# Values' product of two attentions: the two heads of a pair alternate block by block

## The chip, the cores and the metric

One core of a Trainium2 chip runs the kernel. The metric is the device time of one execution in microseconds (us); lower is better. Before the change the median of three runs is 2707.13 us (2704.09 to 2709.62).

## The reference

Two layers on a sequence of 1024 tokens of width 1024, in float32. Each has two token mixers; the change touches one of either layer. In the first layer it is the stick-breaking attention, eight heads of width 64, query blocks of 128:

```
z = jnp.einsum('bhqd,bhkd->bhqk', q[:, :, q0:end], k[:, :, :end]) * scale
mask = kj < qi
log_keep = jnp.where(mask, jax.nn.log_sigmoid(-z), 0.0)
rest = lax.cumsum(log_keep, axis=3, reverse=True) - log_keep
a = jnp.where(mask, jnp.exp(jax.nn.log_sigmoid(z) + rest), 0.0)
outs.append(jnp.einsum('bhqk,bhkd->bhqd', a, v[:, :, :end]))
```

In the second layer it is a softmax attention with low-rank queries and keys, again eight heads with values of width 64:

```
logits = jnp.einsum('bhqd,bhkd->bhqk', qb, k_t).astype(jnp.float32) * scale
logits = jnp.where(allowed[None, None], logits, NEG_INF)
probs = jax.nn.softmax(logits, axis=-1).astype(v_t.dtype)
return jnp.einsum('bhqk,bhkd->bhqd', probs, v_t)
```

Both end in a product of weights and values: the change rewrites how that product is ordered. The rest (a gated delta rule, a differential attention, a gated feed-forward part, projections and norms) stays as it is.

## The kernel before, in words

The program is one list of instructions per engine. A scheduler orders each list when the kernel is built, from the order of the code, the dependencies and its own costs; on the chip every engine works through its list in order. TensorE's order therefore has projections, scores, transposes and values' products mixed.

The stick-breaking attention is `sb` (line 822 on), the softmax attention of the second layer `mla` (line 1159 on). Both call `attend` (line 790), which walks over a list of items from `pairs` (line 885): for each of four pairs of heads `p` and eight query blocks `i`, one item with both heads where `i < 4`, and two items with one head each from `i = 4` on. For item `n`, `attend` first runs `s0` of that item and then `s1` of the item two places earlier. `s0` multiplies queries with keys into a PSUM tile `z` (two of them, each of two banks) and makes the weights: in `sb` three ScalarE passes, a VectorE pass, a VectorE scan, a VectorE subtraction and an exponential, into `cs`; in `mla` a maximum on VectorE, an exponential on ScalarE and a scaling on GpSimd, into `e`. `s1` calls `attend_pv` (line 889), which multiplies the weights with the values.

`attend_pv` needs the weights with keys on the partitions. It transposes them on TensorE, 128 by 128, up to four blocks into one PSUM bank `pt` (line 903), copies the bank to the SBUF tile `aT` (line 904: VectorE in `sb`; in `mla` ScalarE for an item's first chunk and VectorE for the others), and after all chunks of the item multiplies (line 907): 128 keys by 64 value columns as weights, 128 queries streamed. Head 0 of the pair goes to partitions 0 to 63 of the PSUM tile `po`, head 1 to 64 to 127. The blocks are in the order of heads first: all key blocks of head 0, then all of head 1. With `i` 0 or 1 both heads fit one chunk; with `i` 2 and 3 each head has a chunk of its own; from `i = 4` on each head is an item of its own. PSUM's eight banks hold two for projections (`pj`), one `pt`, four for `z` and one `po`.

Beside these attentions `mix` runs a second stream of work: next to `sb` the projections of `proj_z` (512-column products into `pj`), next to `mla_proj` and `mla` the query and key projections of the third attention, `diff_proj`. That one uses `qk_stack` (line 717), whose inner `stack` (line 741) transposes a projected tile (line 747), casts it to `qb_st` on ScalarE and subtracts on VectorE (helper `split_evac`, lines 301 and 302), and stores it to `dr_dqk` (line 750). `qk_stack` runs twice: in `proj_b` in the pool `pb`, and in `diff_proj` in the pool `self.fp`.

Of the kernel before, what the change touches and what calls it, by code (L numbers as in the profile page):

```python
# [11 lines left out]
F32 = mybir.dt.float32  # L12
F32R = mybir.dt.float32r
# [10 lines left out]
NT = 8  # L24
# [127 lines left out]
class Kern:  # L152
# [564 lines left out]
    def qk_stack(self, pool, xn, ws, gains, dst):  # L717


        nc = self.nc  # L720

        def proj(gi, half, w):
            raw = pool.tile([128, 4, 256], F32, tag="qb_raw", name="qb_raw", bufs=2)
            rv = raw.rearrange("p t (h f) -> p (t h) f", h=4)
            ss = pool.tile([128, 16], F32, tag="qb_ss", name="qb_ss", bufs=2)
            for j in range(2):
                ps = self.tm(w, xn, 8, 2 * half + j).rearrange("p j (h f) -> p (j h) f", h=4)
                sq = pool.tile([128, 8, 64], F32, tag="qb_sq", name="qb_sq", bufs=1)
                nc.scalar.activation(sq, ps, AF.Square)
                nc.vector.tensor_tensor(rv[:, 8 * j:8 * j + 8, :], ps, gains[gi // 2][:, None, :].to_broadcast([128, 8, 64]), ALU.mult)  # L730
                nc.vector.reduce_sum(ss[:, 8 * j:8 * j + 8], sq, axis=AX.X)
                yield
            if gi < 2:

                r = self.rsqrt(ss, 16, 1.0, 64 * EPS)
            else:
                r = self.rsqrt(ss, 16, 1.0 / 64, EPS)
            nc.gpsimd.tensor_tensor(rv, rv, r[:, :, None].to_broadcast([128, 16, 64]), ALU.mult)
            self.stack_raw = raw

        def stack(gi, half, raw):
            for pr in range(2):
                p = 2 * (gi % 2) + pr
                st = pool.tile([128, 2, 512], F32R, tag="qb_st", name="qb_st", bufs=2)
                pt = self.PT()
                for j in range(4):
                    nc.tensor.transpose(pt[:, j, :], raw[:, j, pr * 128:pr * 128 + 128], self.ident)
                self.split_evac(st[:, 0], st[:, 1], pt.rearrange("p a b -> p (a b)"))
                a = 2 * (gi // 2)
                nc.sync.dma_start(dst[p, :, a:a + 2, half * 512:half * 512 + 512], st.bitcast(F32))  # L750
                yield

        pend = None
        for gi in range(4):
            w = self.W(ws[gi])
            for half in range(2):
                yield from proj(gi, half, w)
                if pend:
                    yield from stack(*pend)
                pend = gi, half, self.stack_raw  # L760
        yield from stack(*pend)

    def load_qk(self, pool, src, half):
# [58 lines left out]
    def sb(self):  # L822
        nc, d, tc = self.nc, self.d, self.tc
        mm = nc.tensor.matmul
        es = ExitStack()
        sp = es.enter_context(self.pool("sbp", 1, "right"))
        pz = es.enter_context(self.pool("sbz", 2, space=PSUM))
        po_ = es.enter_context(self.pool("sbo", 1, space=PSUM))
        st = {}
# [7 lines left out]
        def s0(p, i, hs):  # L837
# [8 lines left out]
            nk = (i + 1) * 128  # L846
# [3 lines left out]
            for a, h in enumerate(hs):  # L850
                for c0 in range(0, nk, 512):
                    n = min(512, nk - c0)
# [6 lines left out]
            new = lambda tag, bufs: sp.tile([128, 1024], F32, tag=tag, name=tag, bufs=bufs)[:, :len(hs) * nk].rearrange("p (a k) -> p a k", a=len(hs))  # L859
            e = new("e", 2)  # L860
# [2 lines left out]
            nc.scalar.activation(e, e, AF.Exp, scale=-1.0)  # L863
            nc.scalar.activation(e, e, AF.Ln, bias=1.0)
            nc.vector.scalar_tensor_tensor(e, zz, 0.0, e, ALU.max, ALU.add)
            cs = new("cs", 4)
            for a in range(len(hs)):
                nc.vector.tensor_tensor_scan(cs[:, a, ::-1], self.ones[:, 0:1].to_broadcast([128, nk]), e[:, a, ::-1], 0.0, ALU.mult, ALU.add)  # L868
            nc.vector.tensor_tensor(cs, zz, cs, ALU.subtract)
# [1 line left out]
            st[p, i, hs] = cs  # L871

        def s1(p, i, hs):
            cs = st.pop((p, i, hs))
            qk, v, ob = st[p]
            po = self.attend_pv(sp, po_, st, cs, v, i, hs, nc.vector.tensor_copy, nc.vector.tensor_copy)
            if hs[-1] == 1:
                nc.vector.tensor_copy(ob[:, i * 128:i * 128 + 128], po)
                if i == NT - 1:
                    nc.sync.dma_start(self.dr_oa[1, :, p, :], ob)  # L880

        yield from self.attend(self.pairs(), s0, s1)
        es.close()

# [1 line left out]

        return [(p, i, hs) for p in range(4) for i in range(NT) for hs in ([(0, 1)] if i < 4 else [(0,), (1,)])]

    def attend_pv(self, sp, po_, st, e, v, i, hs, *copy):

        nc = self.nc
        mm = nc.tensor.matmul
        if hs[0] == 0:
            st["po"] = po_.tile([128, 128], F32, tag="po", name="po")
        po = st["po"]
        blocks = [(a, j) for a in range(len(hs)) for j in range(i + 1)]
        aT = sp.tile([128, 8, 128], F32, tag="aT", name="aT", bufs=2)
        step = 4 if i != 2 else 3
        for b0 in range(0, len(blocks), step):
            pt = self.PT()  # L900
            bs = blocks[b0:b0 + step]
            for b, (a, j) in enumerate(bs):
                nc.tensor.transpose(pt[:, b, :], e[:, a, j * 128:j * 128 + 128], self.ident)  # L903
            copy[b0 > 0](aT[:, b0:b0 + len(bs), :], pt[:, :len(bs), :])  # L904
        for b, (a, j) in enumerate(blocks):
            h = hs[a]
            mm(po[64 * h:64 * h + 64, :], v[:, j, h * 64:h * 64 + 64], aT[:, b, :], start=j == 0, stop=j == i)  # L907
        return po

    def merge_in(self):  # L910
# [248 lines left out]
    def mla(self):  # L1159
        nc, d, tc = self.nc, self.d, self.tc  # L1160
        mm = nc.tensor.matmul
        es = ExitStack()
        sp = es.enter_context(self.pool("mla", 1, "right"))
        pz = es.enter_context(self.pool("mlaz", 2, space=PSUM))
        po_ = es.enter_context(self.pool("mlao", 1, space=PSUM))
        st = {}
# [14 lines left out]
        def s0(p, i, hs):  # L1181
# [7 lines left out]
            nk = (i + 1) * 128  # L1189
            q = slice(i % 4 * 128, i % 4 * 128 + 128)  # L1190
            z = pz.tile([128, len(hs), 1024 // len(hs)], F32, tag="z", name="z")
            for a, h in enumerate(hs):
                qk = st[p][0]
                qt = qk[h, 0, i // 4]
                for c0 in range(0, nk, 512):
                    n = min(512, nk - c0)
# [5 lines left out]
            zz = z[:, :, :nk]  # L1202
            nm, s, r = (self.small.tile([128, 2], F32, tag=f"a_{n}", name=f"a_{n}", bufs=4)[:, :len(hs)] for n in "msr")
            nc.vector.reduce_max(nm, zz, axis=AX.X, negate=True)
            e = sp.tile([128, 1024], F32, tag="e", name="e", bufs=3)[:, :len(hs) * nk].rearrange("p (a k) -> p a k", a=len(hs))
            for a in range(len(hs)):
                nc.scalar.activation(e[:, a], zz[:, a], AF.Exp, bias=nm[:, a:a + 1], accum_out=s[:, a:a + 1])
            nc.vector.reciprocal(r, s)
# [2 lines left out]
            st[p, i, hs] = e  # L1211

        def s1(p, i, hs):
            e = st.pop((p, i, hs))
            qks, v = st[p]
            po = self.attend_pv(sp, po_, st, e, v, i, hs, nc.scalar.copy, nc.vector.tensor_copy)
            if hs[-1] == 1:
                if i % 4 == 0:
                    st["ob"] = sp.tile([128, 512], F32, tag="ob", name="ob", bufs=1)
                nc.vector.tensor_copy(st["ob"][:, i % 4 * 128:i % 4 * 128 + 128], po)  # L1220
                if i % 4 == 3:
                    nc.sync.dma_start(self.dr_mix[:, p, (i - 3) * 128:(i + 1) * 128], st["ob"])

        yield from self.attend(self.pairs(), s0, s1)
        es.close()

# [448 lines left out]
```

## Time and profile before

| | us |
|---|---|
| median of three runs | 2707.13 |
| lowest, highest | 2704.09, 2709.62 |
| the profiled execution | 2711.15 |
| its span | 2709.3 |
| TensorE matmul busy in the span | 2548.5 (94%) |
| VectorE busy | 1461.3 (54%) |
| ScalarE busy | 864.7 (32%) |
| GpSimd busy | 1057.1 (39%) |
| share of the chain that ended last: TensorE | 61% |

Times of single instructions are from the profiled execution, in us from the start of its span unless marked ns. PE is TensorE's matmul, PEld its weight load, DVE VectorE, ACT ScalarE, POOL GpSimd, SP the engine that issues DMAs. A float32 matmul of the program leaves two records in the trace, one after the other, each with a weight load of its own; the records of a transpose are one each. Matmuls are pipelined, so a record lasts longer than the step to the next: what a matmul costs is read from start to start.

### The profile page before, as it was taken

The numbers are of one execution on the slowest core, as the hardware profiler recorded it, in microseconds if no ns is written. First come the engines' busy times: TensorE is split into PE (matmuls) and PEld (weight loads), VectorE is DVE, ScalarE is ACT, GpSimd is POOL, SyncE is SP. The second block draws the span as 40 slices with busy tenths as digits, with TensorE's granted clock in tenths as the row PEclk, the third lists the DMA queues.
The fourth block names the chain that finished last, engine by engine and source line by source line (L and its number), as shares of the span: only waits on it lengthen the run. The fifth ranks groups of instructions, "written<-read, shape, count | busy, mean of one in ns | idle before, by whom it ended". The sixth has DMA issues, their size and how long they took to land.

```text
span 2709.3 us, 38990 instructions
## 1 busy us (share of the span) xinstructions
PE 2548.5 (94%) x15298; PEld 2173.9 (80%) x15298; DVE 1461.3 (54%) x2837; ACT 864.7 (32%) x1575; POOL 1057.1 (39%) x920
## 2 busy tenths in 40 slices
PE   6998999999999989999889998889999999999999
PEld 6888888877777768989777787788777777777789
DVE  6565565275666554457844336666454454534372
ACT  3322222154444342122324335463333333201031
POOL 2533332122122234544533232223677777634322
PEclk9999999999999999999989999999999999999999
DMA  4433223153421355322674337554122222523222
GB/s 155 132 103 107 79 86 101 56 142 97 119 86 63 133 175 190 105 82 82 207 200 128 94 123 171 170 186 156 55 79 70 86 85 64 196 83 109 70 82 90
DMA packets 152335, 311.46 MB, mean 115 GB/s; under 512 B 14132, under 2 KB 57396, under 8 KB 152152
## 3 DMA queue, kind: packets, MB, share of 16 engines
q1 hardware_dynamic: 152152, 308.97, 36.7%
q8 instruction: 121, 1.98, 0.3%
q14 instruction: 62, 0.51, 0.1%
HBM read 211.91 MB, written 99.37 MB: 115 GB/s over the span
## 4 chain that ended last, share of the span: by engine, by line
PE 61%; DVE 10%; DMA 5%; ACT 3%; issue 2%; POOL 1%; SPq 0%; ACTq 0%; DVEq 0%; POOLq 0%
PE pj L1525 15%; PE pj L254 10%; PE pj L253 10%; PE pj L252 10%; PE po L907 5%; PE pt L903 3%; DMA dr_mla<-l_st 1%; PE po L1333 1%; PE z L253 1%; DVE cs L868 1%; PE z L252 1%; DMA m_o<-dr_oa 1%; DVE rs_a L293 1%; PE z L254 1%; DVE rs_a L292 1%
## 5 line engine op out<-in xcount | busy, mean ns | idle before, releaser
L243 POOL TENSOR_SCALAR hl<-raw 128x512 fp32r<-128x512 f32 (+3 forms) x270 | 197.6, 737 | 961.0 <-PE pj L254 949.5
L244 POOL TENSOR_TENSOR hl<-raw,hl 128x512 fp32r<-128x512 f32 (+3 forms) x270 | 368.7, 1371 | 16.0
L252 PE MATMUL pj<-hl,xn_0h 128*128 128x256 f32 (+2 forms) x544 | 160.6, 296 | 2.3 <-DVE qb_st L302 1.1
L253 PE MATMUL pj<-hl,xn_0h 128*128 128x256 f32 (+2 forms) x544 | 160.6, 295 | 1.7 <-POOL hl L244 1.7
L252 PE MATMUL pj<-hl,xn_1h 128*128 128x256 f32 (+2 forms) x544 | 159.2, 293 | 0.0
L254 PE MATMUL pj<-hl,xn_1l 128*128 128x256 f32 (+2 forms) x544 | 158.8, 292 | 0.0
L254 PE MATMUL pj<-hl,xn_0l 128*128 128x256 f32 (+2 forms) x544 | 158.7, 292 | 0.0
L253 PE MATMUL pj<-hl,xn_1h 128*128 128x256 f32 (+2 forms) x544 | 158.3, 291 | 0.0
L1506 POOL TENSOR_TENSOR hl<-w_s,hl 128x512 fp32r<-128x512 f32 x88 | 120.9, 1375 | 84.1 <-ACT hl L1505 84.0
L907 PE MATMUL po<-aT,v 128*64 128x128 f32 x1152 | 150.4, 280 | 2.2 <-DVE aT L904 1.6
L254 PE MATMUL pj<-hl,f_hl 128*128 128x512 f32 x352 | 140.4, 401 | 2.9 <-DVE f_hl L1607 2.9
L252 PE MATMUL pj<-hl,f_hh 128*128 128x512 f32 x352 | 140.0, 398 | 2.9 <-DVE xres L1616 2.4
L907 PEld LDWEIGHTS po<-aT,v 128*64 128x64 f32 x1152 | 116.5, 136 | 30.6 <-issue 19.2
L253 PE MATMUL pj<-hl,f_hh 128*128 128x512 f32 x352 | 138.3, 393 | 0.0
L1616 DVE TENSOR_TENSOR xres<-xres,pj 128x512 f32<-128x512 f32 x96 | 65.1, 685 | 126.2 <-PE pj L254 113.2
L1506 POOL TENSOR_TENSOR hl<-raw,hl 128x512 fp32r<-128x512 f32 x66 | 100.2, 1524 | 70.4 <-ACT hl L1505 69.7
L904 DVE COPY aT<-pt 128x512 f32<-128x512 f32 (+3 forms) x128 | 72.5, 566 | 99.2 <-PE pt L903 99.0
L1561 DVE TENSOR_TENSOR f_u<-pj,w_u 128x512 f32<-128x512 f32 x44 | 30.4, 692 | 169.1 <-ACT w_u L1529 96.3
L252 PE MATMUL pj<-xn_0h,hl 128*128 128x512 f32 x288 | 116.8, 406 | 0.0
L252 PE MATMUL pj<-xn_1h,hl 128*128 128x512 f32 x288 | 115.7, 402 | 0.0
L254 PE MATMUL pj<-xn_1h,hl 128*128 128x512 f32 x288 | 114.9, 399 | 0.0
L253 PE MATMUL pj<-xn_1l,hl 128*128 128x512 f32 x288 | 114.8, 399 | 0.0
(599 smaller groups left out, 7436.8 us busy)
## 6 DMA issues: line engine op xcount, KB each, us to landing
raw<-in_w_o_dram SPq DMA_DIRECT2D x28, 512.0 KB, 4.3
dr_mla<-l_st SPq DMA_DIRECT2D x32, 384.0 KB, 3.7
qk<-dr_mla SPq DMA_DIRECT2D x32, 384.0 KB, 4.8
raw<-in_w_fg_dram SPq DMA_DIRECT2D x22, 512.0 KB, 4.5
raw<-in_w_fu_dram SPq DMA_DIRECT2D x22, 512.0 KB, 3.5
dr_h<-f_y SPq DMA_DIRECT2D x22, 512.0 KB, 5.3
raw<-in_w_fd_dram SPq DMA_DIRECT2D x22, 512.0 KB, 3.8
f_y<-dr_h SPq DMA_DIRECT2D x22, 512.0 KB, 4.2
```

Of the source, the lines that this page charges most:

```text
L243: nc.gpsimd.tensor_scalar(hl[:, 0], raw[:, k:k + c], 1.0, 1.0, ALU.mult, ALU.mult)
L244: nc.gpsimd.tensor_tensor(hl[:, 1], raw[:, k:k + c], hl[:, 0].bitcast(F32), ALU.subtract)
L252: mm(ps, lh[0], rh[0], start=first, stop=False)
L253: mm(ps, lh[0], rh[1], start=False, stop=False)
L254: mm(ps, lh[1], rh[0], start=False, stop=last)
L903: nc.tensor.transpose(pt[:, b, :], e[:, a, j * 128:j * 128 + 128], self.ident)
L904: copy[b0 > 0](aT[:, b0:b0 + len(bs), :], pt[:, :len(bs), :])
L907: mm(po[64 * h:64 * h + 64, :], v[:, j, h * 64:h * 64 + 64], aT[:, b, :], start=j == 0, stop=j == i)
L1506: nc.gpsimd.tensor_tensor(hl[:, 1], v, hl[:, 0].bitcast(F32), ALU.subtract)
L1525: nc.tensor.matmul(ps, w[k][l], b[r][:, k, :], start=first and k + n == 0, stop=k == 3 and n == 2, skip_group_check=not first)
L1561: nc.vector.tensor_tensor(u, ps, v, ALU.add)
L1616: nc.vector.tensor_tensor(xr, xr, ps, ALU.add)
```

## The change

`attend_pv` takes both heads of a pair at once. Where the heads are items of their own, `s1` does nothing for the first and handles both with the second. The loop goes over key blocks two at a time; a chunk holds those two blocks of both heads, head 0 and head 1 in turn, in one PSUM bank. Each chunk has its own small `aT` tile (four blocks; five buffers in `sb`, four in `mla`, where there were two of eight blocks), and its products follow directly in the code, again with heads in turn. Since more weights are held at a time, `cs` goes from four to five buffers and `e` of `mla` from three to four; to make room, `qb_st` has one buffer in the pool `self.fp` and still two in the other. The line numbers move by one or two: 903 becomes 904 and 907 becomes 908.

```diff
         def stack(gi, half, raw):
...
-                st = pool.tile([128, 2, 512], F32R, tag="qb_st", name="qb_st", bufs=2)
+                st = pool.tile([128, 2, 512], F32R, tag="qb_st", name="qb_st", bufs=1 if pool is getattr(self, "fp", None) else 2)
...
-            cs = new("cs", 4)
+            cs = new("cs", 5)
...
         def s1(p, i, hs):
-            cs = st.pop((p, i, hs))
+            if hs == (0,):
+                return
             qk, v, ob = st[p]
-            po = self.attend_pv(sp, po_, st, cs, v, i, hs, nc.vector.tensor_copy, nc.vector.tensor_copy)
-            if hs[-1] == 1:
-                nc.vector.tensor_copy(ob[:, i * 128:i * 128 + 128], po)
+            po = self.attend_pv(sp, po_, st, v, p, i, 5, nc.vector.tensor_copy, nc.vector.tensor_copy)
+            nc.vector.tensor_copy(ob[:, i * 128:i * 128 + 128], po)
...
-    def attend_pv(self, sp, po_, st, e, v, i, hs, *copy):
+    def attend_pv(self, sp, po_, st, v, p, i, bufs, *copy):
         nc = self.nc
-        mm = nc.tensor.matmul
-        if hs[0] == 0:
-            st["po"] = po_.tile([128, 128], F32, tag="po", name="po")
-        po = st["po"]
-        blocks = [(a, j) for a in range(len(hs)) for j in range(i + 1)]
-        aT = sp.tile([128, 8, 128], F32, tag="aT", name="aT", bufs=2)
-        step = 4 if i != 2 else 3
-        for b0 in range(0, len(blocks), step):
+        if i < 4:
+            both = st.pop((p, i, (0, 1)))
+            e = [both[:, a] for a in range(2)]
+        else:
+            e = [st.pop((p, i, (a,)))[:, 0] for a in range(2)]
+        po = po_.tile([128, 128], F32, tag="po", name="po")
+        for j0 in range(0, i + 1, 2):
+            blocks = [(j, a) for j in range(j0, min(j0 + 2, i + 1)) for a in range(2)]
+            n = len(blocks)
             pt = self.PT()
-            bs = blocks[b0:b0 + step]
-            for b, (a, j) in enumerate(bs):
-                nc.tensor.transpose(pt[:, b, :], e[:, a, j * 128:j * 128 + 128], self.ident)
-            copy[b0 > 0](aT[:, b0:b0 + len(bs), :], pt[:, :len(bs), :])
-        for b, (a, j) in enumerate(blocks):
-            h = hs[a]
-            mm(po[64 * h:64 * h + 64, :], v[:, j, h * 64:h * 64 + 64], aT[:, b, :], start=j == 0, stop=j == i)
+            for b, (j, a) in enumerate(blocks):
+                nc.tensor.transpose(pt[:, b, :], e[a][:, j * 128:j * 128 + 128], self.ident)
+            aT = sp.tile([128, 4, 128], F32, tag="aT", name="aT", bufs=bufs)
+            copy[j0 > 0](aT[:, :n], pt[:, :n])
+            for b, (j, a) in enumerate(blocks):
+                nc.tensor.matmul(po[64 * a:64 * a + 64, :], v[:, j, a * 64:a * 64 + 64], aT[:, b, :], start=j == 0, stop=j == i)
         return po
...
-            e = sp.tile([128, 1024], F32, tag="e", name="e", bufs=3)[:, :len(hs) * nk].rearrange("p (a k) -> p a k", a=len(hs))
+            e = sp.tile([128, 1024], F32, tag="e", name="e", bufs=4)[:, :len(hs) * nk].rearrange("p (a k) -> p a k", a=len(hs))
...
         def s1(p, i, hs):
-            e = st.pop((p, i, hs))
+            if hs == (0,):
+                return
             qks, v = st[p]
-            po = self.attend_pv(sp, po_, st, e, v, i, hs, nc.scalar.copy, nc.vector.tensor_copy)
-            if hs[-1] == 1:
...
+            po = self.attend_pv(sp, po_, st, v, p, i, 4, nc.scalar.copy, nc.vector.tensor_copy)
```

The scheduler's order changes with it. TensorE in `sb`, near query block 6 of the first pair, before (`pj` is a projection product, `pt` a chunk of transposes, `po` values' products; x4 counts matmuls of the program):

```order
L252 MATMUL pj<-xn_0h,hl 128x512
L903 MATMUL pt<-cst,cs 128x128 x3
L907 MATMUL po<-aT,v 64x128 x4
L253 MATMUL pj<-xn_0l,hl 128x512
L254 MATMUL pj<-xn_0h,hl 128x512
L252 MATMUL pj<-xn_0h,hl 128x512
L907 MATMUL po<-aT,v 64x128 x3
```

and now:

```order
L904 MATMUL pt<-cst,cs 128x128 x4
L252 MATMUL pj<-xn_1h,hl 128x512
L253 MATMUL pj<-xn_1l,hl 128x512
L254 MATMUL pj<-xn_1h,hl 128x512
L252 MATMUL pj<-xn_1h,hl 128x512
L908 MATMUL po<-aT,v 64x128 x4
L904 MATMUL pt<-cst,cs 128x128 x4
```

Before, the products of one head's chunks stand in runs of up to eight matmuls; now a run is one chunk of four (or two), with four or five projection products between its transposes and its products.

TensorE at the end of `mla` (`z` are the scores, `identb` loads the weights for the mask's product), now:

```order
L904 MATMUL pt<-cst,e 128x128 x4
L252 MATMUL z<-qk 128x512
L253 MATMUL z<-qk 128x512
L254 MATMUL z<-qk 128x512
L1202 LDWEIGHTS identb
L1202 MATMUL z<-negch,identb 128x64
L908 MATMUL po<-aT,v 64x128 x4
L904 MATMUL pt<-cst,e 128x128 x4
L908 MATMUL po<-aT,v 64x128 x4
L904 MATMUL pt<-cst,e 128x128 x4
```

Three score products and a mask stand between transposes and products, and after the last scores nothing does. Before, projection products of the next phase stand in this place.

ScalarE in the first pair of `qb_st` casts beside `mla_proj`, before:

```order
L301 CAST qb_st<-pt 128x512 x2
L304 ACTIVATE qlT0h<-pt,g_ql 128x512 x2
L304 ACTIVATE kvT0h<-pt,g_kvl 128x512
L729 ACTIVATE qb_sq<-pj 128x512
```

and now:

```order
L301 CAST qb_st<-pt 128x512
L304 ACTIVATE qlT0h<-pt,g_ql 128x512 x2
L304 ACTIVATE kvT0h<-pt,g_kvl 128x512
L301 CAST qb_st<-pt 128x512
L729 ACTIVATE qb_sq<-pj 128x512
```

The second cast has moved behind three other evictions, ahead of `qb_sq`.

## Rows read from the trace of the kernel before

**Rows 1.** Busy us of each engine by stretch, with counts; granted clock, DMA share, GB/s.

```profile
554.00:914.00 360.00, 353.58 (x1949) 272.91 (x1948) 240.56 (x293) 162.57 (x203) 77.15 (x72) 1.00 0.32 93
1230.00:1413.00 183.00, 156.04 (x1151) 148.60 (x1150) 130.64 (x344) 56.01 (x117) 79.22 (x64) 0.94 0.57 169
1413.00:1628.00 215.00, 212.22 (x1501) 170.68 (x1501) 85.88 (x178) 83.09 (x190) 63.82 (x82) 0.99 0.39 117
```

**Rows 2.** The chain of waits by line, at 554 to 914, then 1413 to 1628.

```profile
by line: PE po L907 18.2%; PE pj L253 15.2%; PE pj L254 15.0%; PE pj L252 14.6%; PE pt L903 8.8%; DVE cs L868 5.3%; PE z L855 4.1%; PE z L856 4.0%; DVE e L865 2.8%; issue 2.1%; ACT e L862 1.9%; ACT e L864 1.7%; DVE cs L869 1.5%; DVE aT L904
...
by line: PE po L907 32.2%; PE pt L903 17.8%; PE z L253 9.0%; PE z L252 8.3%; PE z L254 7.4%; PE pj L253 5.2%; PE pj L252 4.9%; PE pj L254 4.8%; DMA dr_mix<-ob 2.4%; PE z L1201 1.5%; POOL hl L244 1.2%; POOL hl L243 1.1%; PE pt L747 1.0%; ACT
```

**Rows 3.** Instructions by shape, 554 to 914: records | busy us, mean ns | idle before.

```profile
L907 PE MATMUL po<-aT,v 128*64 128x128 f32 x576 | 75.5, 280 | 1.6 <-DVE aT L904 1.6
```

**Rows 4.** Timeline, one head's run and a copy: start, length, engine, instruction, records.

```profile
572.11 0.60 PE L903 MATMUL pt<-cst,cs 128*128 128x128 f32 x4
572.64 1.09 PE L907 MATMUL po<-aT,v 128*64 128x128 f32 x8
573.66 0.39 PE L856 MATMUL z<-k,q 128*128 128x256 f32 x1
...
572.75 0.69 DVE L904 COPY aT<-pt 128x512 f32<-128x512 f32 x1 [0.65 <-PE pt L903]
```

**Rows 5.** Timeline of TensorE, the runs of query blocks 0 and 1.

```profile
555.91 0.44 PE L907 MATMUL po<-aT,v 128*64 128x128 f32 x4
556.28 0.50 PE L252 MATMUL pj<-xn_1h,hl 128*128 128x512 f32 x1
...
559.35 0.40 PE L252 MATMUL pj<-xn_1h,hl 128*128 128x512 f32 x1
559.58 0.39 PE L253 MATMUL pj<-xn_1l,hl 128*128 128x512 f32 x1
559.90 0.66 PE L907 MATMUL po<-aT,v 128*64 128x128 f32 x8
560.50 0.50 PE L254 MATMUL pj<-xn_1h,hl 128*128 128x512 f32 x1
```

**Rows 6.** Timeline of the weight loads of the two runs of eight.

```profile
559.90 0.42 PEld L907 LDWEIGHTS po<-aT,v 128*64 128x64 f32 x8 [0.36 <-issue]
...
572.64 0.85 PEld L907 LDWEIGHTS po<-aT,v 128*64 128x64 f32 x8 [0.17 <-issue]
```

**Rows 7.** Copies of four blocks, by shape: 554 to 914, then 1413 to 1628.

```profile
L904 DVE COPY aT<-pt 128x512 f32<-128x512 f32 x52 | 35.7, 686 | 32.3 <-PE pt L903 32.2
...
L904 ACT COPY aT<-pt 128x512 f32<-128x512 f32 x40 | 23.4, 586 | 73.5 <-PE pt L903 68.2 <-issue 3.7 <-PE z L1201 1.6
```

**Rows 8.** Waits on the copies, us, times, longest: 554 to 914, then 1413 to 1628.

```profile
PEld pt L903 <- DVE aT L904: 11.9, 28, 1.3
PEld po L907 <- DVE aT L904: 4.3, 8, 1.3
PE pt L903 <- DVE aT L904: 3.6, 6, 0.9
...
PEld pt L903 <- ACT aT L904: 6.5, 25, 0.5
PE pt L903 <- ACT aT L904: 1.1, 3, 0.4
```

**Rows 9.** Casts and stores of `qb_st`, timeline; last the DMA's median us to landing.

```profile
1237.28 1.07 ACT L301 CAST qb_st<-pt 128x512 fp32r<-128x512 f32 x2
...
1241.42 0.94 SPq L750 DMA_DIRECT2D dr_dqk<-qb_st  x2
...
1260.71 0.36 SPq L750 DMA_DIRECT2D dr_dqk<-qb_st  x1
...
1261.24 0.59 ACT L301 CAST qb_st<-pt 128x512 fp32r<-128x512 f32 x1 [2.00 <-PE pt L747]
...
dr_dqk<-qb_st SPq DMA_DIRECT2D x16, 512.0 KB, 4.4
```

More of the change, by code (lines that the diff above doesn't have):

```diff
@@ L873, in s1 @@
         def s1(p, i, hs):
-            cs = st.pop((p, i, hs))
+            if hs == (0,):
+                return
             qk, v, ob = st[p]
-            po = self.attend_pv(sp, po_, st, cs, v, i, hs, nc.vector.tensor_copy, nc.vector.tensor_copy)
-            if hs[-1] == 1:
-                nc.vector.tensor_copy(ob[:, i * 128:i * 128 + 128], po)
-                if i == NT - 1:
-                    nc.sync.dma_start(self.dr_oa[1, :, p, :], ob)
+            po = self.attend_pv(sp, po_, st, v, p, i, 5, nc.vector.tensor_copy, nc.vector.tensor_copy)
+            nc.vector.tensor_copy(ob[:, i * 128:i * 128 + 128], po)
+            if i == NT - 1:
+                nc.sync.dma_start(self.dr_oa[1, :, p, :], ob)
         yield from self.attend(self.pairs(), s0, s1)
@@ L1213, in s1 @@
         def s1(p, i, hs):
-            e = st.pop((p, i, hs))
+            if hs == (0,):
+                return
             qks, v = st[p]
-            po = self.attend_pv(sp, po_, st, e, v, i, hs, nc.scalar.copy, nc.vector.tensor_copy)
-            if hs[-1] == 1:
[L1218 to L1222, printed above, removed]
+            po = self.attend_pv(sp, po_, st, v, p, i, 4, nc.scalar.copy, nc.vector.tensor_copy)
+            if i % 4 == 0:
+                st["ob"] = sp.tile([128, 512], F32, tag="ob", name="ob", bufs=1)
+            nc.vector.tensor_copy(st["ob"][:, i % 4 * 128:i % 4 * 128 + 128], po)
+            if i % 4 == 3:
+                nc.sync.dma_start(self.dr_mix[:, p, (i - 3) * 128:(i + 1) * 128], st["ob"])
         yield from self.attend(self.pairs(), s0, s1)
```

## The prediction

> **What bounds the kernel now.** I read the stretches first, then the chain of waits in the two that hold the change, then the instructions one by one. The two attentions whose values' products are rewritten run at 554 to 914 us (stick-breaking, function `sb`) and 1413 to 1628 us (`mla`). In both, TensorE is busy for 98 to 99% of the stretch at a granted clock of 1.00 and 0.99, VectorE for 67% and 40%, ScalarE for 45% and 39% [rows 1]. The chain agrees: the largest single item is the values' product itself, L907, with 18.2% of 360 us (65.5 us) and 32.2% of 215 us (69.2 us) [rows 2]. TensorE's time saved there is time saved, as long as the copies that feed it keep up. In 1230 to 1413 us, where the other edit (one `qb_st` buffer) falls, no engine is full: TensorE 156 and VectorE 131 of 183 us [rows 1].
>
> **How long a values' product takes.** The program has 576 of them (two attentions, eight heads, 36 blocks each); the trace holds 2 records for each, 576 per attention [rows 3], so counts of records below are twice the matmuls. A matmul of one head fills 64 of the 128 output partitions. Eight records of one head, at 572.64, last 1.02 us up to the next instruction (573.66); the whole run lasts 1.09 us, so seven steps and a last record of 0.28 us: about 0.11 us a record [rows 4]. At 559.90 stand eight records too, but there both heads' matmuls for query block 1 come out of one copy: next instruction at 560.50, 0.60 us later, the run 0.66 us, so about 0.055 us a record. Query block 0, four records of two heads, takes 0.37 us [rows 5]. **Two heads in one run take half the time per record**; the kernel before has this only at blocks 0 and 1, because from block 2 on each head has its own chunk and so its own run.
> Here a rule of the Trainium skill speaks against the change. The weight loads of the two-head run start at 559.90 with its matmuls and need 0.42 us, against 0.85 us for one head [rows 6], so the loads of one head run beside the other's matmuls. The Trainium skill (TensorE: Matmul & The Clock Gate, Part 3: Packing small matmuls) says that a weight load overlaps matmuls in flight only when it targets other rows of the array; both heads use all 128 rows. By that rule nothing would overlap and the change would only add runs (third rival). The trace disagrees at blocks 0 and 1.
>
> **The sum on TensorE.** Besides its records a run costs what surrounds it. Before: 1.02 - 8 x 0.11 is 0.14 us, and the step into it is 0.32 us after a 512-column product (559.58 to 559.90) where 0.23 is normal (559.35 to 559.58) [rows 5]: 0.09 more, 0.24 us a run.
> - Before: the order has 71 and 69 runs. 48 matmuls of blocks 0 and 1 (96 records) already overlap, 1056 records don't: 1056 x 0.109 + 96 x 0.055 + 140 x 0.24 = 115.1 + 5.3 + 33.6 = 154 us.
> - After: 16 chunks of four matmuls and 4 of two for each pair of heads, so 128 and 32 in all, nearly each a run of its own (159 in the order): 128 x (0.60 + 0.09) + 32 x (0.37 + 0.09) = 88.3 + 14.7 = 103 us.
> - Difference: **-51 us**, half in each attention. Transposes (576) and their columns stay the same.
>
> **What it costs.** *Copies.* 176 copies become 160 with the same columns in all: nothing. But chunks follow one another more closely. From the first of four transposes to the end of their copy takes 1.33 us (572.11 to 573.44) [rows 4], with 0.69 us for the copy on VectorE and 0.59 on ScalarE [rows 7]. Counted from where the next matmul could start (572.55) that leaves 0.89 us, some 0.95 by estimate with the signal to TensorE, to fill, once ahead of the chunk's products and, as these stretches have one `pt` bank, once ahead of the next transposes. The new order puts four 512-column products there in `sb` (4 x 0.23 = 0.92, just enough) and in `mla` often three and a mask (some 0.75), at the end nothing but transposes and products in turn. Short by 0.05 us on 80 chunks and by 0.2 on 80: 20 us. The same count on the order before gives about 10. So +10 us. The larger measured waits on these copies are 20 us in `sb` and 8 in `mla` before [rows 8]. Bounds: 0 (the products now wait for their own chunk alone), and 36 (the whole 16 us of `mla`'s shortness, and the 20 us of `sb` again, since a copy there also queues behind VectorE's scans, and TensorE outruns it sooner).
> *`qb_st` with one buffer*, in `diff_proj` alone: 16 tiles, 12 of them beside `mla_proj`. The second cast of a pair must now wait until the first tile's store has landed. At 1237.28 two casts follow each other; the store is issued at 1241.42 and takes 4.4 us: 1245.8 instead of 1237.8, 8.0 us later. At 1261.24 it is 1260.71 + 4.4, so 3.9 us later [rows 9]. The mean of the two on six pairs is 36 us, the upper end; the lower is 0. ScalarE's order now has three to six other instructions between the casts, and it idles there (56 of 183 us busy [rows 1]); what stands behind the cast (`qb_sq`, `l_sq`, and VectorE's subtraction with all behind it) loses about 1 us a pair: +5 us. The last four tiles, beside `mla`, stand five to eight rows apart in ScalarE's order: nothing.
> *Moved and held.* Both heads' products now wait for the second head's turn; `cs` goes from 4 to 5 buffers and `e` from 3 to 4, as many as are held at most, so the score tiles don't wait: nothing. If it did, the next scores would be late by a chain of ScalarE and VectorE.
> Total: -51 + 10 + 5 = **-36 us**. The profiled execution took 2711.15 us, so 2675; the median of the runs is 4.0 us lower, so **2671 us**.
>
> **Rivals.**
> 1. *The wait takes the gain's place:* TensorE gets through its products, then stands at the copies. For: the covers above are at their limit, and `sb` already waits 20 us. Against: VectorE has 119 of 360 us free. At the upper bound, -51 + 36 + 5 = -10 us: 2697.
> 2. *The single `qb_st` buffer holds the projections up:* every wait reaches the path. For: in-order ScalarE and VectorE. Against: the moved casts. -51 + 10 + 36 = -5 us: 2702.
> 3. *Slower: no overlap when heads alternate block by block.* Blocks 0 and 1 are the only evidence, in runs of at most four matmuls. If the 159 runs keep 0.11 us a record, blocks 0 and 1 lose theirs too: 19 x 0.24 + 96 x 0.054 + 10 + 5 = +25 us: 2732. It decides from a record interval of about 0.088 us upward, where 1152 records and the costs eat the gain. Against: the new chunk is the same two blocks by two heads as block 1's run. The rule of the Trainium skill on weight loads (TensorE: Matmul & The Clock Gate, Part 3) would bring this about.
>
> **How the numbers follow.** Forecast 0.77, rival 1 0.13, rival 2 0.06, rival 3 0.04. The forecast's own bounds run from 2656 (no cost) to about 2692. The range 2654 to 2696 leaves out most of rival 1 and rivals 2 and 3. A measurement here can tell about 0.2%, 5.4 us, from no change. Faster by more than that: nearly all of the forecast, most of rival 1, half of rival 2: 0.91. Within: 0.05. Slower: 0.04.
>
> **What would show it.** Right: runs of eight records of the values' product at 0.60 to 0.66 us throughout, their share of the chain down by about two fifths; the `sb` stretch shorter by some 22 us, `mla` by some 18; 1230 to 1413 longer by a few us with ScalarE waiting for `dr_dqk<-qb_st`. Wrong: runs of 1.0 us (rival 3); waits of the transposes or products for `aT` above 60 us in both stretches together (rival 1); waits on `qb_st` of 20 us or more that TensorE shares (rival 2).

## The result, and the profile after

The changed kernel takes **2680.5 us** (median of four runs, 2677.5 to 2685.0), the kernel before 2708.4 in the same comparison: a ratio of 0.989, interval 0.9876 to 0.9903, so 28 us faster. The forecast was 36 us and the range holds the result.

First the time by stretch. Windows of equal times would cut the two kernels at different work, so these run from work to work: from the first score product of the first attention (`sb`) to its last values' product; from the first latent projection of `mla_proj` to the first score product of `mla`; and from there to the first product of `ple_proj`, which takes in `mla`, the output projection that is interleaved with it and the third attention (`diff`). Columns as in [rows 1]. The kernel before:

```profile
546.50:914.07 367.57, 360.98 (x1987) 278.79 (x1985) 242.61 (x297) 166.32 (x211) 81.22 (x77) 1.00 0.33 95
1181.11:1409.09 227.98, 199.34 (x1420) 191.22 (x1419) 154.35 (x426) 62.78 (x133) 99.92 (x84) 0.96 0.46 140
1409.09:1762.41 353.32, 329.74 (x2321) 273.60 (x2322) 176.03 (x467) 150.55 (x378) 99.05 (x115) 0.97 0.50 140
```

The changed kernel, the same view:

```profile
548.48:901.24 352.76, 334.78 (x1987) 248.38 (x1985) 240.27 (x289) 166.70 (x211) 81.82 (x77) 1.00 0.35 101
1164.76:1389.76 225.00, 198.93 (x1420) 190.50 (x1419) 149.88 (x426) 62.82 (x133) 100.20 (x84) 0.97 0.46 141
1389.76:1730.12 340.36, 303.03 (x2322) 246.70 (x2322) 186.23 (x475) 141.29 (x362) 100.56 (x115) 0.94 0.53 146
```

Length less TensorE's busy time is TensorE's idle time, and that splits each difference:

| stretch | length | TensorE busy | TensorE idle |
|---|---|---|---|
| `sb` | -14.8 | -26.2 | +11.4 |
| `mla_proj` | -3.0 | -0.4 | -2.6 |
| `mla` to `ple_proj` | -13.0 | -26.7 | +13.7 |

The three make -30.8; the stretches between and after them add 0.9 (+2.0 ahead of `sb`, -3.5 between `sb` and `mla_proj`, +2.4 after), and the span is 29.9 us shorter (2679.4 against 2709.3). So TensorE does its work 53 us faster, as forecast (51), and 25 us of that come back as idle time in two places.

The busy time first. Instructions by shape, 548 to 901.5, answering to [rows 3]:

```profile
L908 PE MATMUL po<-aT,v 128*64 128x128 f32 x576 | 49.7, 289 | 16.7 <-DVE aT L906 15.9 <-DVE ob L878 0.5
```

TensorE's timeline around a run deep in a row, answering to [rows 4] and [rows 5]:

```profile
620.70 0.61 PE L904 MATMUL pt<-cst,cs 128*128 128x128 f32 x4
621.07 0.48 PE L252 MATMUL pj<-xn_1h,hl 128*128 128x512 f32 x1
...
621.84 0.39 PE L252 MATMUL pj<-xn_1h,hl 128*128 128x512 f32 x1
622.16 0.66 PE L908 MATMUL po<-aT,v 128*64 128x128 f32 x8
622.75 0.66 PE L904 MATMUL pt<-cst,cs 128*128 128x128 f32 x4
```

Eight records now take 0.59 us to the next instruction (622.16 to 622.75), which before only block 1 did; of the 80 runs of `sb`, the 64 with eight records have a median of 0.588 us. The same 576 records have 49.7 us of busy time where they had 75.5.

Now the idle time. Waits for the copies, 548 to 902, answering to [rows 8]:

```profile
PE po L908 <- DVE aT L906: 15.9, 20, 1.8
...
PEld po L908 <- DVE aT L906: 42.2, 73, 2.2
```

And one of them, on VectorE and TensorE together:

```profile
607.75 0.60 PE L904 MATMUL pt<-cst,cs 128*128 128x128 f32 x4
...
608.71 2.29 DVE L868 TENSOR_TENSOR_SCAN cs<-ones,e 128x1024 f32<-128x1024 f32 x1
610.91 0.67 DVE L906 COPY aT<-pt 128x512 f32<-128x512 f32 x1
...
611.63 0.66 PE L908 MATMUL po<-aT,v 128*64 128x128 f32 x8 [1.76 <-DVE aT L906]
```

The transposes start at 607.75, but VectorE begins a scan of 2.29 us at 608.71, the copy stands behind it, and TensorE idles 1.76 us. The chain in `sb` says the same, answering to [rows 2]: the scan (`cs` L868), 5.3% before, is now its largest item, and the values' product fell from 18.2 to 9.3%.

```profile
by line: DVE cs L868 15.7%; PE po L908 9.3%; DVE e L865 7.8%; PE pj L254 7.7%; PE pj L252 7.2%; PE pj L253 7.2%; PE pt L904 6.9%; DVE cs L869 5.7%; DVE aT L906 5.5%; issue 4.6%; ACT e L864 3.8%; ACT e L863 3.3%; ACT e L862 3.3%; DMA dr_oa<-
```

The other place is behind `mla`. TensorE's waits, 1389.8 to 1611:

```profile
PE z L1302 <- DMA q<-dr_dqk: 10.1, 1, 10.1
PE po L908 <- DVE aT L906: 5.2, 8, 0.8
...
PE po L908 <- ACT aT L906: 2.2, 4, 0.7
```

The largest wait has nothing to do with a copy: TensorE stands 10.1 us for the first `q` tile of the third attention. SP's timeline of the kernel before, where this wait is absent, shows how it was covered:

```profile
1593.38 0.91 SPq L1363 DMA_DIRECT2D m_o<-dr_mix  x2
...
1603.10 15.21 SPq L1363 DMA_DIRECT2D m_o<-dr_mix  x4
...
1630.94 0.37 SPq L1250 DMA_DIRECT2D lam<-in_lam_dram  x1
...
1632.40 0.60 SPq L772 DMA_DIRECT2D q<-dr_dqk  x1
```

The same issues in the changed kernel:

```profile
1581.86 0.38 SPq L1251 DMA_DIRECT2D lam<-in_lam_dram  x1
...
1584.37 0.60 SPq L772 DMA_DIRECT2D q<-dr_dqk  x1
...
1594.33 3.52 SPq L1364 DMA_DIRECT2D m_o<-dr_mix  x2
```

Before, the loads of `mla`'s output (`m_o`, for the output projection) went out ahead of `lam` and `q`, and the output projection ran beside `mla`'s end. Now they come after, and TensorE has nothing to do between `mla` and `diff`. The first experiments ask what makes the runs short and what moved these loads.

### The profile page after: what moved, and what is told of

Same layout as the page of the kernel before. It is cut to its first block, busy times and chain, and to the rows that moved or that the text cites. A ratio compares the mean times of both kernels' runs of the same rounds, so it can differ in the third digit from the quotient of the medians.

```text
span 2679.4 us, 38930 instructions
## 1 busy us (share of the span) xinstructions
PE 2500.3 (93%) x15298; PEld 2120.9 (79%) x15298; DVE 1466.8 (55%) x2837; ACT 855.9 (32%) x1559; POOL 1060.5 (40%) x920
## 4 chain that ended last, share of the span: by engine, by line
PE 57%; DVE 12%; DMA 5%; ACT 4%; issue 3%; POOL 1%; SPq 0%; DVEq 0%; ACTq 0%; POOLq 0%
PE pj L1526 15%; PE pj L254 10%; PE pj L252 10%; PE pj L253 10%; PE po L908 3%; PE pt L904 2%; DVE cs L868 2%; DVE e L865 1%; DVE aT L906 1%; PE po L1334 1%; DMA m_o<-dr_oa 1%; DVE cs L869 1%; PE z L252 1%; DVE rs_a L292 1%; DVE rs_a L293 1%
## 5 line engine op out<-in xcount | busy, mean ns | idle before, releaser
L906 DVE COPY aT<-pt 128x512 f32<-128x512 f32 (+1 forms) x128 | 80.4, 628 | 107.6 <-PE pt L904 100.3
L908 PE MATMUL po<-aT,v 128*64 128x128 f32 x1152 | 98.7, 288 | 25.8 <-DVE aT L906 21.1
L252 PE MATMUL pj<-xn_0h,hl 128*128 128x512 f32 x288 | 117.3, 407 | 0.0
L908 PEld LDWEIGHTS po<-aT,v 128*64 128x64 f32 x1152 | 60.0, 136 | 71.9 <-DVE aT L906 52.7
L254 PE MATMUL pj<-xn_0h,hl 128*128 128x512 f32 x288 | 115.1, 400 | 0.0
```

The source lines that it names most:

```text
L252: mm(ps, lh[0], rh[0], start=first, stop=False)
L254: mm(ps, lh[1], rh[0], start=False, stop=last)
L906: copy[j0 > 0](aT[:, :n], pt[:, :n])
L908: nc.tensor.matmul(po[64 * a:64 * a + 64, :], v[:, j, a * 64:a * 64 + 64], aT[:, b, :], start=j == 0, stop=j == i)
```

## Experiments on the cause

**e1: is it the halves?** From block 1 on both heads write `po[0:64]`.

```diff
-                nc.tensor.matmul(po[64 * a:64 * a + 64, :], v[:, j, a * 64:a * 64 + 64], aT[:, b, :], start=j == 0, stop=j == i)
+                w = 64 * a if j == 0 else 0
+                nc.tensor.matmul(po[w:w + 64, :], v[:, j, a * 64:a * 64 + 64], aT[:, b, :], start=j == 0, stop=w == 64 or i == 0 or (j == i and a == 1))
```

> The changed kernel, but from the second key block of a row on both heads accumulate into the first 64 output columns of po (the second head's own half gets block 0 alone), so that what is accumulated differs from the reference; number, order and size of the products stay as in the changed kernel. Theory A (products overlap because consecutive ones go to different column halves): 512 of the 576 product records of each attention lose their overlap and go from 0.055 to 0.109 us, 28 us for each attention; the runs of eight records take 0.9 to 1.0 us from first to next instead of 0.588, and the span is 35 to 55 us longer than the changed kernel's 2679. Theory B (it is the alternation of weights and moving tiles, or the chunks of two blocks, that makes the runs short, not the halves): runs stay at 0.55 to 0.65 us and the span within 5 us of 2679.

Measured: 2719.8 us in one run, span 2718.0, 38.6 over the changed kernel. A run deep in a row, TensorE's timeline of e1:

```profile
619.18 1.09 PE L909 MATMUL po<-aT,v 128*64 128x128 f32 x8
620.20 0.44 PE L904 MATMUL pt<-cst,cs 128*128 128x128 f32 x2
```

1.02 us again, as for one head before [rows 4], with the alternation, the chunks and the weights of the changed kernel. (A row's first run, where block 0 of each head still has its own half, takes 0.80.) `sb` is 25.0 us longer than in the changed kernel (377.78), TensorE's waits for `aT` on PE are 16.6 us instead of 15.9. Block 1 on means 448 of an attention's 576 records, not the 512 of the expectation; at 0.054 us each that is 24 us, and TensorE's busy time in `sb` rises by 24.1 (358.85 against 334.78). Theory A: what halves the time is that the two heads write different halves of `po`, not their order or their chunks. But in e1 both heads also add to the same sums, and e11 separates the two:

**e11: the same half, no sums.** Each product is a group of its own, and the heads write to two places of the bank.

```diff
-                w = 64 * a if j == 0 else 0
-                nc.tensor.matmul(po[w:w + 64, :], v[:, j, a * 64:a * 64 + 64], aT[:, b, :], start=j == 0, stop=w == 64 or i == 0 or (j == i and a == 1))
+                w, c = (64 * a, 0) if j == 0 else (0, a)
+                nc.tensor.matmul(po2[w:w + 64, c, :], v[:, j, a * 64:a * 64 + 64], aT[:, b, :], start=True, stop=True)
```

> As e1 (from block 1 on both heads' products go to the first 64 output columns), but no product accumulates onto another: each is a group of its own, and the two heads write to two different places of the bank. What is left out is the sum over key blocks. Theory A (the shared thing is the 64 columns of the array and their output partitions): runs deep in a row stay at 1.0 us as in e1, the span at 2700 to 2725. Theory B (in e1 the products waited because they accumulated into the same place): runs fall to 0.55 to 0.65 us and the span to within 5 us of 2679.

Measured: 2725.2 us in one run, span 2723.4. TensorE's timeline of e11:

```profile
620.03 1.09 PE L910 MATMUL po<-aT,v 128*64 128x128 f32 x8
621.05 0.66 PE L905 MATMUL pt<-cst,cs 128*128 128x128 f32 x4
```

1.02 us without any sum over key blocks: theory A, it is the half itself. (Columns of the array and partitions of the output go together here; which of the two it is, no run tells.)

**e4: must heads alternate?** Within a chunk, first head 0's two blocks, then head 1's.

```diff
-            for b, (j, a) in enumerate(blocks):
+            for b, (j, a) in sorted(enumerate(blocks), key=lambda x: x[1][1]):
```

> The changed kernel with the products of a chunk in the order head 0 block 0, head 0 block 1, head 1 block 0, head 1 block 1 instead of heads taking turns. Theory A (products of two halves overlap as soon as both are in the queue of the array, some records deep): runs of eight stay at 0.55 to 0.65 us, span within 5 us of 2679. Theory B (only neighbours overlap): six of the eight records have their own half as neighbour, runs of eight take 0.8 to 0.95 us, and the span is 15 to 30 us longer.

Measured: 2681.9 us in one run, span 2680.1. TensorE's timeline of e4:

```profile
626.08 0.66 PE L908 MATMUL po<-aT,v 128*64 128x128 f32 x8
626.68 0.66 PE L904 MATMUL pt<-cst,cs 128*128 128x128 f32 x4
```

0.60 us. Theory A: the two halves overlap although, in the code's order, four records of one head stand ahead of the other's. The kernel before had shown it: its run of block 1 [rows 5] is heads first too.

How far apart the halves may stand, the kernel before also shows. In block 3 of three of the four pairs of `sb` both heads' products make one run, eight records of head 0 and then eight of head 1. TensorE's timeline before, a run of one head (block 7, at 621.41) and one of both heads (block 3, at 658.16):

```profile
621.41 1.96 PE L907 MATMUL po<-aT,v 128*64 128x128 f32 x16
623.30 0.50 PE L254 MATMUL pj<-xn_0h,hl 128*128 128x512 f32 x1
...
658.16 1.94 PE L907 MATMUL po<-aT,v 128*64 128x128 f32 x16
660.03 0.50 PE L253 MATMUL pj<-xn_0l,hl 128*128 128x512 f32 x1
```

1.89 us for one head and 1.87 for both: next to no overlap. So the change's "turns block by block" is not needed, but the two heads have to be near: two products of one head ahead of the other's are few enough (e4), four are too many.

**e2: the `qb_st` buffer alone**, in the kernel before.

```diff
-                st = pool.tile([128, 2, 512], F32R, tag="qb_st", name="qb_st", bufs=2)
+                st = pool.tile([128, 2, 512], F32R, tag="qb_st", name="qb_st", bufs=1 if pool is getattr(self, "fp", None) else 2)
```

> The kernel before with one part of the change alone: one qb_st buffer instead of two where the projections of the second attention use it. Theory A (ScalarE's and VectorE's waits for the store stay inside their slack, since TensorE bounds that stretch): no difference, within 5 us of the kernel before. The prediction's term: 5 us longer. Theory B (the wait for the landing of each store is passed on to TensorE): up to 36 us longer, with the projections' stretch longer by as much and ScalarE's qb_st groups ended by the store's DMA.

Measured: 2710.5 us against 2708.8, ratio 1.0007 (0.9996 to 1.0018). ScalarE does wait for the store, in e2's stretch 1180 to 1410:

```profile
ACT qb_st L301 <- DMA dr_dqk<-qb_st: 7.1, 3, 3.6
```

But it idles there (62.85 of 225.8 us busy), and the stretch is 225.8 us long where it was 228.0. Theory A: the wait is real, and no cost shows (the interval is -1 to +5 us).

**e9: the buffers alone.** e2, and four instead of three `e` buffers in `mla`. One `qb_st` tile and one `e` tile are both 4 KB per partition (1024 float32), so the first edit makes the room for the second.

```diff
-            e = sp.tile([128, 1024], F32, tag="e", name="e", bufs=3)[:, :len(hs) * nk].rearrange("p (a k) -> p a k", a=len(hs))
+            e = sp.tile([128, 1024], F32, tag="e", name="e", bufs=4)[:, :len(hs) * nk].rearrange("p (a k) -> p a k", a=len(hs))
```

> The kernel before with the change's buffers alone and its products' order as before: one qb_st buffer in the second attention's projections (which by e2 costs nothing) and, in the room that this leaves, four instead of three e buffers in the second attention, so that its pool is 4 KB per partition larger, as in the changed kernel. Theory A (the larger pool alone pushes the output projection's tiles onto the attention's memory): the m_o loads come behind lam and the next attention's loads, their first products start after the attention and not 20 us before its end, TensorE waits some 10 us for the first q load, and the time is 8 to 14 us over the kernel before, near 2720. Theory B (the order came from the attention's shorter time): as the kernel before, within 4 us.

Measured: 2721.8 us against 2710.5, ratio 1.0044 (1.0027 to 1.006): 11 us slower, with the products as before. In the profiles the stretch from `mla` to `ple_proj` is 361.73 us long where it was 353.32, 8.4 us more. SP's issues in e9:

```profile
1625.36 0.39 SPq L1250 DMA_DIRECT2D lam<-in_lam_dram  x1
...
1627.80 0.60 SPq L772 DMA_DIRECT2D q<-dr_dqk  x1
```

Its six `m_o` loads of that time begin at 1637.7, and its output projection at 1655.0 (1605.9 before). TensorE's waits in e9, 1409 to 1760, begin with the same row as the changed kernel's:

```profile
PE z L1301 <- DMA q<-dr_dqk: 10.1, 1, 10.1
```

**e3: the same from the other side.** The changed kernel with `mla`'s pool as small as before: two `aT` buffers (2 KB each) instead of four.

```diff
-            po = self.attend_pv(sp, po_, st, v, p, i, 4, nc.scalar.copy, nc.vector.tensor_copy)
+            po = self.attend_pv(sp, po_, st, v, p, i, 2, nc.scalar.copy, nc.vector.tensor_copy)
```

> The changed kernel with two instead of four aT buffers in the second attention, which makes that attention's pool 4 KB per partition smaller, as large as before the change. Theory A (the 4 KB more put the tiles of the output projection, mixo, on memory that the second attention holds to its end, so that its loads, and with them its products, come behind the attention, and TensorE stands about 10 us for the first q load of the next attention): the m_o loads are issued ahead of the attention's last products again, TensorE's wait for the q load (10.1 us) is gone or under 3 us, and the time is 8 to 12 us below the changed kernel's 2680, near 2670. Theory B (the q load is late because the attention itself ends earlier, not because of memory): the order of the loads and the 10 us wait stay, and the time is 2680 or, if two aT buffers hold the copies back, up to 10 us more.

Measured: 2668.1 us, ratio 0.9838 (0.9817 to 0.9859): 12 us below the changed kernel, whose interval lies clear of this one. The issues in e3 stand in the old order:

```profile
1558.33 1.55 SPq L1364 DMA_DIRECT2D m_o<-dr_mix  x2
...
1563.91 13.19 SPq L1364 DMA_DIRECT2D m_o<-dr_mix  x4
...
1590.96 0.37 SPq L1251 DMA_DIRECT2D lam<-in_lam_dram  x1
...
1595.60 0.60 SPq L772 DMA_DIRECT2D q<-dr_dqk  x1
```

The wait for `q` is 1.7 us instead of 10.1, TensorE's waits for `aT` in `mla` are 1.6 us instead of 7.4, and the stretch from `mla` to `ple_proj` 327.64 us instead of 340.36, with 25.8 us idle where the kernel before had 23.6:

```profile
1393.18:1720.82 327.64, 301.88 (x2322) 245.89 (x2322) 185.67 (x475) 140.17 (x362) 99.21 (x115) 0.97 0.55 152
```

Theory A in both: 4 KB per partition in `mla`'s pool decide whether the output projection may start beside `mla` or only behind it, and that is worth 11 to 12 us. That its tiles then share memory with `mla`'s is concluded from the order of the loads; no view shows addresses.

## Experiments on the copies' waits

All start from e3. Compared are the times, `sb`'s length (352.73 us in e3) and TensorE's waits for `aT` there (16.0 us on PE in e3). Medians of four or five executions that lie 3 to 4 us apart can't be told from each other, so the stretch is the better witness, though it is that of one execution: where `sb` is the same, its length agrees between traces (367.57 us before and 367.58 in e9, 352.76 in the changed kernel and 352.73 in e3).

**e5: the first copy of each row on ScalarE.**

```diff
-            po = self.attend_pv(sp, po_, st, v, p, i, 5, nc.vector.tensor_copy, nc.vector.tensor_copy)
+            po = self.attend_pv(sp, po_, st, v, p, i, 5, nc.scalar.copy, nc.vector.tensor_copy)
```

> The kernel of e3 (2668 us) with the first copy of each item in the first attention on ScalarE instead of VectorE. Theory A (the products wait for aT because the copies stand behind scans of 1 to 2.3 us in VectorE's queue; ScalarE is busy 167 of 353 us there, VectorE 240): TensorE's waits for aT in the stretch 546 to 903, 16 us on PE and 42 on PEld, fall to about 8 and 25, and the time is 4 to 9 us below 2668. Theory B (the wait is the latency of transposes, copy and semaphores, whoever copies): the waits move from VectorE to ScalarE with the same sum, and the time stays within 3 us of 2668.

Measured: 2664.4 us, ratio 0.9828 (0.9813 to 0.9842). TensorE's waits in `sb`:

```profile
PE po L908 <- DVE aT L906: 6.5, 10, 1.0
PE po L908 <- ACT aT L906: 3.8, 7, 1.4
```

10.3 us instead of 16.0, `sb` 350.6 us long, 2.1 shorter. On PE the waits fall by about two thirds of what theory A gave, on PEld from 42.3 to 35.5 where it gave 25. The time, 3.6 us below e3's, lies between what the two theories gave and doesn't decide.

**e6: a chunk's products behind the next chunk's transposes.**

```diff
+            if late:
+                products(*late)
             aT = sp.tile([128, 4, 128], F32, tag="aT", name="aT", bufs=bufs)
             copy[j0 > 0](aT[:, :n], pt[:, :n])
-            for b, (j, a) in enumerate(blocks):
-                nc.tensor.matmul(po[64 * a:64 * a + 64, :], v[:, j, a * 64:a * 64 + 64], aT[:, b, :], start=j == 0, stop=j == i)
+            late = blocks, aT
+        products(*late)
```

> The kernel of e3 (2668 us) with the products of a chunk of two blocks issued after the transposes of the next chunk of the same row, in both attentions, the last chunk's right behind it. Theory A (copies late against the products): the waits for aT in the first attention fall from 16 us on PE to 5 to 10, and the time is 5 to 10 us below 2668. Theory B (the planner already puts projection products between the transposes and the products, and only fills other places with them when the next transposes stand there): same waits within 4 us, and the time within 4 us of 2668; with less projection work between a transpose and its products, longer waits and up to 10 us more.

Measured: 2667.5 us, ratio 0.9832 (0.9816 to 0.9849). Waits in `sb`:

```profile
PE pt L909 <- DVE aT L913: 7.5, 13, 1.7
...
PE po L901 <- DVE aT L913: 1.0, 2, 0.8
```

Half of the wait is gone, as theory A says, and what is left stands at the transposes, which need the one `pt` bank back. The time is theory B's, for a reason that neither named: `sb` is 352.1 us long with 4.99 us more of TensorE's busy time (339.74 against 334.75). From transposes to a 512-column product the median step is 0.028 us, from transposes to a values' product 0.202; e6 puts 48 runs straight behind transposes where e3 had 4: 44 x 0.17 = 7.5 us, less 38 steps from a 512-column product into a run that it saves (29 against 67) at 0.1, 3.8. That is 3.7 of the 5 us.

**e7: four blocks by two heads in `sb`** (two copies, then up to eight products; two `aT` tiles of eight blocks in place of five of four).

```diff
-        for j0 in range(0, i + 1, 2):
...
+        for j1 in range(0, i + 1, w):
+            aT = sp.tile([128, 2 * w, 128], F32, tag="aT", name="aT", bufs=bufs)
```

> The kernel of e3 (2668 us) with chunks of four key blocks by two heads in the first attention (two groups of transposes with two copies, then up to eight products with the heads in turn), the second attention as in e3. 80 runs of products become 48. Theory A (each run pays an entry and an exit of about 0.2 us beside its products): 32 times 0.2 is 6 us of TensorE's time, and the time is 3 to 8 us below 2668, if the waits for aT stay at 16 us. Theory B (both copies of a group must be there before its products can follow one another, so waits grow by what the runs save): within 3 us of 2668 or up to 8 us more.

Measured: 2664.9 us, ratio 0.9827 (0.9803 to 0.9851). The runs stayed: the scheduler puts projection work between the products of the first two blocks and of the last two, and the trace still has 64 runs of eight records and 16 of four (two of them follow another with a wait of 0.20 us between). Waits for `aT` on PE fall to 9.8 us, TensorE's busy time grows by 4.8, and `sb` is 354.3 us long, 1.5 more. So this says nothing of the price of a run.

**e8: e5 and e6 together.**

> The kernel of e3 (2668 us) with both e5's and e6's edits. Theory A (both take away the same wait for the copies): as the better of e5 and e6, within 3 us. Theory B (they take away different waits, the copy's place in VectorE's queue and its distance from the products): the sum of what the two gain, 2655 or below.

Measured: 2664.1 us, ratio 0.9825 (0.981 to 0.9839); `sb` 346.6 us, 6.2 less than e3, more than the 2.1 of e5 and the 0.6 of e6 together. The stretch speaks for theory B, that the two take away different waits; the time, 4 us below e3's, fits theory A and doesn't reach B's 2655.

**e10: e8 with all copies of `sb` on ScalarE.**

> The kernel of e8 (2664 us) with all copies of the first attention on ScalarE, none on VectorE. Theory A (what waits are left there come from VectorE's scans ahead of the copies): the waits <-DVE aT, 2.8 us on PE in e8, go, and the time is 2 to 4 us below e8's. Theory B (two engines share the copies better than one; ScalarE's own row of Exp and Ln, of 167 us with 353, stands ahead of the copies instead): the waits <-ACT aT grow by as much or more, and the time is within 2 us of e8's or up to 5 us over it.

Measured: **2655.7 us**, ratio 0.9805 (0.9789 to 0.9822), the lowest median of all. `sb`, and its waits:

```profile
546.50:891.37 344.87, 336.51 (x1987) 251.23 (x1985) 195.25 (x209) 199.66 (x291) 80.68 (x77) 1.00 0.37 103
```

```profile
PE pt L909 <- ACT aT L913: 4.9, 9, 0.9
...
PE po L901 <- ACT aT L913: 0.8, 1, 0.8
```

The waits for VectorE are gone and those for ScalarE grew: 5.7 us, as much as e8's 5.4 in all, so theory B for the waits. The time, 8 us below e8's, is in neither theory's range. `sb` is 1.7 us shorter than in e8. The profile of e10 is 7.2 us shorter than e8's, but 5.1 of these lie ahead of `sb`, in work that no edit touches. Against the changed kernel e10's interval is clear; how much of the 8 us to e8 is its own edit stays open.

## Why the prediction was right, and where it was off

*The sum on TensorE, -51.* Right in size and cause. TensorE's busy time fell by 26.2 and 26.7 us. The forecast counted 128 runs at 0.60 and 32 at 0.37 with 0.09 to enter each; the runs have medians of 0.588 and 0.37, and the step from a 512-column product into one is 0.327 where 0.23 is normal. One reason that it gave doesn't hold: from block 2 on, it says, each head has a run of its own. In block 3 the heads mostly share a run, and what keeps it long is that four products of one head stand ahead of the other's (1.87 us for 16 records).

*Copies, +10.* The number is near, partly by luck: the cause named was the right one, but not where and how it acts. Its sign in `sb`, some 22 us shorter, came as 14.8, with the chain's share of the values' product halved. There idle time grew by 11.4 us; e3, whose hand-over is as before, has 2.2 us more idle time from `mla` to `ple_proj`. Together 13.6. The forecast had the covers short by 0.05 us on each of the 80 chunks in `sb` and by 0.2 in `mla`. It was the other way round: with the old hand-over (e3) `mla` loses little, and in `sb` it is not a small lack on each chunk but 20 waits of up to 1.8 us, where a copy falls behind a scan. VectorE's queue appeared only in the upper bound. e5, e8 and e10 bear it out: with the copies on ScalarE TensorE waits less.

*`qb_st`, +5.* No cost shows in e2; its interval, -1 to +5 us, reaches just to the term, and the stretch that was to grow is 2 to 3 us shorter in e2 and in the changed kernel. The prediction itself had the reason: ScalarE idles for two thirds of that stretch and other instructions stand between the casts.

*Moved and held: nothing.* **This is the step that failed.** The prediction asked of the fourth `e` buffer only whether score tiles would wait, not what the 4 KB per partition that it adds to `mla`'s pool would displace. They cost 11 (e9) to 12 us (e3), more than either of the two costs that the prediction weighed. Without them the forecast of 2671 would have been 3 us above the 2668 of e3: too high for the `qb_st` term, too low for the copies. That the result lies only 8 us from the forecast is in part luck: 12 us that were not foreseen stand against 5 us that didn't come.

*The rivals.* Rival 1 had waits for `aT` above 60 us in both stretches as its mark, and by the letter that was met: 15.9 + 42.2 us in `sb`, and in `mla` 7.4 on PE and 18.6 on PEld, 84 us together. The mark was badly chosen. A wait on PEld runs beside matmuls still in flight; PE's own waits are 23.3 us. Rival 2 falls with e2. Rival 3 falls with the runs of 0.588 us, and e1 shows what it would have looked like: runs of 1.02 us and a span 8.6 us over the kernel before. The rule of the Trainium skill (TensorE: Matmul & The Clock Gate, Part 3: Packing small matmuls), by which a weight load overlaps matmuls in flight only towards other rows, isn't borne out as a reason against the change: both heads use all 128 rows in e1 and in the changed kernel, and the half that they write makes the difference, 1.02 or 0.59 us for eight records. That section also lists small matmuls packed by output columns as running at once, and this the traces bear out.

## What to carry to other kernels

Matmuls that fill only half of the output partitions should be queued near others that fill the other half: here two of one kind ahead of two of the other were near enough, four ahead of four were not. Every buffer that a change adds must be paid from somewhere: find what is allocated next in that memory and whether it used to start before the owner was done. And when an engine is made faster, look at the queue of the one that feeds it: an instruction of 2.3 us ahead of a short copy becomes the wait.

## What was not expected of the hardware

The hand-over costs more than its wait of 10.1 us. TensorE by stretch in the changed kernel, from the end of `mla`:

```profile
1581.00:1591.20 10.20, 0.08 (x2) 0.01 (x1) 1.24 (x6) 0.20 (x1) 0.00 (x0) 0.50 0.76 170
1591.20:1601.20 10.00, 4.27 (x15) 3.13 (x15) 1.47 (x11) 1.48 (x6) 0.00 (x0) 0.50 1.08 240
1601.20:1611.20 10.00, 8.26 (x33) 5.38 (x34) 7.35 (x33) 6.46 (x21) 0.00 (x0) 0.66 0.60 152
1611.20:1626.00 14.80, 14.80 (x118) 14.03 (x118) 13.75 (x35) 9.38 (x23) 3.36 (x4) 1.00 0.73 196
```

While TensorE stands, the granted clock is 0.50, the lower of its two levels (1.2 of 2.4 GHz), and it is still there for the first 10 us of work and part of the next 10. In e3, where the output projection fills the gap, the clock over the corresponding 33 us (1589.2 to 1622.6) is 1.00 throughout. Before, the same place had one window of 10 us at 0.83. What the clock alone costs no run separates. Over the whole stretch from `mla` to `ple_proj` TensorE's busy time is only 1.2 us more than in e3 (303.03 against 301.88) and its idle time 11.6 us more; the waits for `q` (8.4 more) and for `aT` in `mla` (5.8 more) cover that.

And which kind follows which on TensorE has a price: a step takes 0.20 us from transposes into a values' product or from one back to transposes, against 0.03 from transposes to a 512-column product (medians in `sb` of e6). By the count under e6 it makes most of the busy time that ate what e6 saved in waits.
